# A and B on the sync queue behind the first group of x, B on 32 partitions, and one copy moved: what a shorter setup chain is worth in a LoRA kernel

## Chip, cores and metric

The kernel runs on one core of a Trainium2 chip. The metric is the device time of one execution in microseconds (us). An execution more than 1.5% above the fastest of the same kernel is labelled slow and left out.

## The reference

```python
# x [16, 512, 768], A [768, 16], B [16, 768], all float32; scale = 0.5
lora = np.matmul(np.matmul(x, A), B)
return (x + scale * lora).astype(np.float32)
```

25.2 MB of x come in and 25.2 MB of output go out. A and B have 48 KB each.

## The kernel before

The 8192 rows of x go through in eight groups of 1024. Each partition holds 8 consecutive rows of a group, so a group is 128 pieces of 24,576 bytes. The first six groups are loaded at once into six buffers. The last two wait until stores have freed a buffer. All loads and stores of x are issued on the sync queue (SP), one after another. In the trace of before they land in that order: the loads of the third to the sixth group, issued between 1.39 and 3.17 us, landed 24.2, 30.8, 37.5 and 44.4 us after their issue.

```python
def sync_program():
    ...
    load(0)            # moved into the first block, ahead of the barrier that all engines share
    ...
    for g in range(1, X_BUFS):          # X_BUFS = 6
        load(g)
    for g in range(NG - 1):             # NG = 8
        nc.sync.wait_ge(added, 4 * (g + 1) + 2)
        nc.sync.dma_start(out=view(out2, g), in_=xs[g % X_BUFS]).then_inc(...)
        if g == len(freed) - 1:         # after the second store
            for n in range(X_BUFS, NG):
                nc.sync.wait_ge(freed[n - X_BUFS], 16)
                load(n)
    ...
# last of all:
nc.sync.dma_start(out=view(out2, NG - 1), in_=xs[(NG - 1) % X_BUFS])
```

Per group, ACT casts x to float16, DVE transposes it, PE multiplies by a block form of A (24 matmuls into `y_ps`, "a y pass"), ACT spreads y into diagonal blocks, PE multiplies these by B, and DVE adds the result to x in place.

Before the first group a setup brings A and B into their block forms. A and B are loaded by ACT, behind the barrier:

```python
def scalar_program():
    nc.scalar.dma_start(out=a32, in_=A.rearrange("(p m q) r -> p m (q r)", m=NM, q=2)
                        ).then_inc(a_in, 16)
    nc.scalar.dma_start(out=b32, in_=B).then_inc(b_in, 16)
    ...

def vector_program():
    nc.vector.wait_ge(pool_done, 4)
    nc.vector.tensor_tensor(out=a16, in0=..., in1=..., op=mult     # A, masked
                            )._wait_ge(a_in, 16).then_inc(setup_dve, 1)
    nc.vector.tensor_copy(out=b16[0:R, :], in_=b32)._wait_ge(b_in, 16).then_inc(setup_dve, 1)
    for a in range(NQ): ...            # four copies from PSUM to a_diag
    nc.vector.tensor_copy(out=b_rep, in_=b_ps)._wait_ge(setup_pe, 3).then_inc(added, 2)
    turn(0, 0, G // 2)._wait_ge(ready, 1)          # the first two transposes
    turn(0, G // 2, G // 2)._wait_ge(ready, 2)
    for g in range(NG):
        if g + 1 < NG:
            turn(g + 1, 0, G)._wait_ge(ready, 2 * g + 4)
        for s in range(0, G, 2): ...   # four adds, then the group can be stored
```

Of the kernel before, what the change touches and what calls it, by code (L numbers as in the profile page):

```python
# [1 line left out]

# [7 lines left out]
MM_DT = mybir.dt.float16  # L10
# [4 lines left out]
Q = 32  # L15
# [3 lines left out]
def kernel(  # L19
# [14 lines left out]
    nc = tc.nc  # L34
    fp32 = mybir.dt.float32
    u32 = mybir.dt.uint32
    P = 128
    NQ = P // Q
# [3 lines left out]
    T, D = x2.shape  # L42
    R = A.shape[1]
# [3 lines left out]
    NB = W // Q  # L47
    NM = 4
    PB, PA = Q // NM, W // NM
    assert PA <= P and NM * P <= 512  # L50
    sc = float(scale)

    const = ctx.enter_context(tc.tile_pool(name="const", bufs=1))
    psum = ctx.enter_context(tc.tile_pool(name="psum", bufs=1, space=bass.MemoryType.PSUM))


    x_0 = nc.alloc_sbuf_tensor("x_0", [P, G, D], fp32).ap()
    xs = [x_0] + [const.tile([P, G, D], fp32, name=f"x_{i}") for i in range(1, X_BUFS)]
    xh = [const.tile([P, G, D], MM_DT, name=f"xh_{i}") for i in range(2)]
    xt = const.tile([P, G, W], u32, name="xt")  # L60
    y_diag = const.tile([P, G, P], MM_DT, name="y_diag")


    a32 = const.tile([PA, NM, 2 * R], fp32, name="a32")
    mine = const.tile([PA, NB], MM_DT, name="mine")
    wrap = const.tile([PB, PA], MM_DT, name="wrap")
    step = const.tile([PB, NM, NQ, Q], MM_DT, name="step")
    sel = const.tile([PA, NM, P], MM_DT, name="sel")
    b32 = const.tile([R, D], fp32, name="b32")
    rep = const.tile([Q, NQ * Q], MM_DT, name="rep")  # L70
    a16 = const.tile([PA, NM, NB, 2 * R], MM_DT, name="a16")
    b16 = const.tile([Q, D], MM_DT, name="b16")
    a_diag = const.tile([P, 2 * NB, P], MM_DT, name="a_diag")
    b_rep = const.tile([P, D], MM_DT, name="b_rep")
    y_ps = psum.tile([P, G, Q], fp32, name="y_ps")
    lora_ps = [psum.tile([P, 2, D], fp32, name=f"lora_ps_{i}") for i in range(2)]
# [8 lines left out]
    a_in, b_in = semaphore("a_in"), semaphore("b_in")  # L85
# [17 lines left out]
    def load(g):  # L103
        nc.sync.dma_start(out=xs[g % X_BUFS], in_=view(x2, g)).then_inc(loaded[g], 16)

    def sync_program():
        symbolic, nc._always_lower_symbolic_ap = nc._always_lower_symbolic_ap, False
        load(0)
        nc._always_lower_symbolic_ap = symbolic

        now, first = nc.cur_bb.bb.instructions, nc.main_func.blocks[0].instructions
        at = next(
            k for k, i in enumerate(first)
            if i.engine == mybir.EngineType.SP and isinstance(i, mybir.InstDrain)
        )
        first.insert(at, now.pop())
        for g in range(1, X_BUFS):
            load(g)
        for g in range(NG - 1):
            nc.sync.wait_ge(added, 4 * (g + 1) + 2)  # L120
            nc.sync.dma_start(out=view(out2, g), in_=xs[g % X_BUFS]).then_inc(
                freed[g] if g < len(freed) else stored, 16
            )
            if g == len(freed) - 1:
# [4 lines that stand above are left out]
        nc.sync.wait_ge(added, 4 * NG + 2)  # L129
        nc.sync.sem_clear(range(nums[0], nums[-1] + 1))  # L130

    def pool_program():
        nc.gpsimd.sem_clear(stored)

        nc.gpsimd.memset(rep, 0.0)
        nc.gpsimd.memset(wrap, 0.0)
        nc.gpsimd.memset(step, 0.0)
        nc.gpsimd.memset(mine, 1.0).then_inc(pool_done, 1)
        nc.gpsimd.affine_select(
            out=rep.rearrange("i (a k) -> i a k", a=NQ),  # L140
            in_=rep.rearrange("i (a k) -> i a k", a=NQ),
            compare_op=mybir.AluOpType.not_equal, fill=1.0, base=0,
            pattern=[[0, NQ], [-1, Q]], channel_multiplier=1,
        )._wait_ge(pool_done, 1)

        nc.gpsimd.affine_select(
            out=wrap.rearrange("j (b k) -> j b k", k=PB),
            in_=wrap.rearrange("j (b k) -> j b k", k=PB),
            compare_op=mybir.AluOpType.not_equal, fill=1.0, base=0,
            pattern=[[0, NB], [-1, PB]], channel_multiplier=1,  # L150
        )

        nc.gpsimd.affine_select(
            out=step, in_=step,
            compare_op=mybir.AluOpType.not_equal, fill=1.0, base=0,
            pattern=[[1, NM], [0, NQ], [-1, Q]], channel_multiplier=NM,
        )

        nc.gpsimd.affine_select(
            out=mine, in_=mine, compare_op=mybir.AluOpType.is_ge, fill=0.0, base=0,  # L160
            pattern=[[-PB, NB]], channel_multiplier=1,
        ).then_inc(pool_done, 1)
        nc.gpsimd.affine_select(
            out=mine, in_=mine, compare_op=mybir.AluOpType.is_ge, fill=0.0, base=PB - 1,
            pattern=[[PB, NB]], channel_multiplier=-1,
        )._wait_ge(pool_done, 2).then_inc(pool_done, 1)
        nc.gpsimd.memset(b16, 0.0)
        nc.gpsimd.memset(a_diag, 0.0)
        nc.gpsimd.memset(y_diag, 0.0).then_inc(pool_done, 1)

# [4 lines left out]
        return i  # L175

    def scalar_program():
        nc.scalar.dma_start(
            out=a32, in_=A.rearrange("(p m q) r -> p m (q r)", m=NM, q=2)
        ).then_inc(a_in, 16)  # L180
        nc.scalar.dma_start(out=b32, in_=B).then_inc(b_in, 16)

        nc.scalar.copy(out=sel.rearrange("p m k -> p (m k)"), in_=sel_ps)._wait_ge(
            setup_pe, 1
        ).then_inc(setup_act, 1)
        cast(0, 0, G // 2)._wait_ge(loaded[0], 16)
        cast(0, G // 2, G // 2)
        cast(1, 0, G)._wait_ge(loaded[1], 16)
        for g in range(NG):
            for a in range(NQ):  # L190
                q = ds(a * Q, Q)
                i = nc.scalar.mul(out=y_diag[q, :, q], in_=y_ps[q, :, :], mul=sc)  # L192
                if a == 0:
                    i._wait_ge(ready, min(g + 3, NG + 1) + g + 1)
            i.then_inc(spread, 1)
            if g + 2 < NG:
                cast(g + 2, 0, G)._wait_ge(loaded[g + 2], 16)

    a_ps = lora_ps[0][:, 0, 0 : 2 * NB * R]
    b_ps = lora_ps[1][:, 0, :]  # L200
    sel_ps = lora_ps[0].rearrange("p s d -> p (s d)")[0:PA, 512 : 512 + NM * P]

    def turn(g, s0, n):
        rows = ds(s0, n)
        i = nc.vector.transpose(  # L205
            out=xt[:, rows, :].rearrange("p s w -> p (s w)"),
            in_=xh[g % 2][:, rows, :].rearrange("p s d -> p (s d)").bitcast(u32),
        )
        i.then_inc(turned, 1)
        return i  # L210

    def vector_program():
        nc.vector.wait_ge(pool_done, 4)
        nc.vector.tensor_tensor(  # L214
            out=a16,
            in0=a32[:, :, None, :].to_broadcast([PA, NM, NB, 2 * R]),
            in1=mine[:, None, :, None].to_broadcast([PA, NM, NB, 2 * R]),
            op=mybir.AluOpType.mult,
        )._wait_ge(a_in, 16).then_inc(setup_dve, 1)
        nc.vector.tensor_copy(  # L220
            out=b16[0:R, :], in_=b32
        )._wait_ge(b_in, 16).then_inc(setup_dve, 1)
        for a in range(NQ):
            q = ds(a * Q, Q)
            i = nc.vector.tensor_copy(  # L225
                out=a_diag[q, :, ds(a * Q, R)], in_=a_ps[q, :].rearrange("p (b r) -> p b r", r=R)
            )
            if a == 0:
                i._wait_ge(setup_pe, 2)
        nc.vector.tensor_copy(out=b_rep, in_=b_ps)._wait_ge(setup_pe, 3).then_inc(added, 2)  # L230
        turn(0, 0, G // 2)._wait_ge(ready, 1)
        turn(0, G // 2, G // 2)._wait_ge(ready, 2)
        for g in range(NG):
            if g + 1 < NG:
                turn(g + 1, 0, G)._wait_ge(ready, 2 * g + 4)
            for s in range(0, G, 2):
                n = (g * G + s) // 2
                rows = xs[g % X_BUFS][:, ds(s, 2), :]
                nc.vector.tensor_tensor(  # L239
                    out=rows, in0=rows, in1=lora_ps[n % 2], op=mybir.AluOpType.add  # L240
                )._wait_ge(ups, n + 1).then_inc(added, 1)

    def chunks(c0, n):

        while n:
            k = min(n, 512 - c0 % 512)
            yield c0, k
            c0, n = c0 + k, n - k

    def tensor_program():  # L250
# [9 lines left out]
            if m == 0:  # L260
                i._wait_ge(setup_dve, 1)
        i.then_inc(setup_pe, 1)
        for c0, n in chunks(0, D):
            i = nc.tensor.matmul(
                b_ps[:, ds(c0, n)], rep, b16[:, ds(c0, n)], start=True, stop=True
            )
            if c0 == 0:
                i._wait_ge(setup_dve, 2)
        i.then_inc(setup_pe, 1)
        xt_mm = xt.rearrange("p s w -> p (s w)").bitcast(MM_DT)  # L270
# [69 lines left out]
```

## Time and profile before

| | before |
|---|---|
| time, median of 3 runs | 123.38 us (123.22 to 123.45) |
| span of the profiled run | 121.6 us |
| busy: DVE / ACT / PE | 70% / 46% / 44% |
| sync queue, share of the 16 DMA engines' span | 97.3% |
| last store issued | 109.83 us |

First the page of the kernel before: the DMA rows over the span in 40 slices (tenths busy, then GB/s), the queues (packets, MB, share of the 16 engines), the chain of waits by engine, and one of the issue lines (count, KB each, median us from issue to landing).

```profile
span 121.6 us, 908 instructions
...
DMA  7999999999999999999999999999999999999990
GB/s 234 407 405 409 437 445 404 445 445 404 445 445 404 445 429 421 396 485 412 396 493 404 404 485 404 412 461 421 429 445 412 437 445 412 437 445 412 445 437 40
...
q1 hardware_dynamic: 2304, 50.33, 97.3%
q10 hardware_dynamic: 144, 0.10, 0.3%
...
DVE 51%; PE 28%; DMA 9%; ACT 1%; issue 1%; ACTq 0%; SPq 0%
...
out_dram<-x_61 SPq DMA_DIRECT2D x2, 3072.0 KB, 12.3
```

Queue q1 is the sync queue, q10 is ACT's. The DMA engines are at 9 tenths or more in every slice but the first and the last. The chain of waits nevertheless names DVE and PE and gives the DMA engines 9%. How can both be true? The chain is followed back from the last piece of computing work, and that is the last add. These are its final pieces (start, us, what):

```profile
101.72 0.83 PE lora_ps_82 L289 x4
102.58 6.75 DVE x_61 L239 x4
```

It ends at 109.3 us, and the page follows nothing beyond. The last store and its landing, the remaining 12 us, are not part of it. So this chain says what the last store waits for before it is issued. Here is the issue of the last store (start, us taken, engine, line), then the sync queue's wait for its landing (us in total, times, longest):

```profile
109.83 0.33 SPq L304 DMA_DIRECT2D out_dram<-x_61  x1
...
SPq L335 <- DMA out_dram<-x_61: 10.6, 1, 10.6
```

Last, the setup on DVE from the timeline (start, us, what, and in brackets the idle time before it and what ended it), and below the dots the first y pass on PE:

```profile
11.44 1.75 DVE L214 TENSOR_TENSOR a_77<-a_70,mine 96x1536 f16<-96x1536 f32 x1 [11.44 <-DMA a_70<-in_A_dram]
13.73 0.55 DVE L220 CAST b_78<-b_75 16x768 f16<-16x768 f32 x1 [0.55 <-DMA b_75<-in_B_dram]
14.74 2.26 DVE L225 CAST a_diag<-lora_ps_82 32x384 f16<-32x384 f32 x4 [0.46 <-PE lora_ps_82 L256]
17.01 0.96 DVE L230 CAST b_rep<-lora_ps_83 128x768 f16<-128x768 f32 x1
17.89 3.43 DVE L205 STREAM_TRANSPOSE xt<-xh_66 128x1536 uint32<-128x1536 uint32 x2
...
21.37 5.20 PE L275 MATMUL y_ps<-xt,a_diag 128*128 128x256 f16 x24 [5.92 <-DVE xt L205]
```

So the first y matmul starts at 21.37 us.

### The profile page before, as it was taken

To read this page: it belongs to the slowest core of one execution; us is meant where nothing else is said; L and a number is where in the kernel's file an instruction comes from. 1 tells how busy PE (TensorE), PEld (TensorE's weight loads), DVE (VectorE), ACT (ScalarE), POOL (GpSimd) and SP (SyncE) were. 2 spreads that over 40 slices of the span, in tenths; PEclk is the share of its full clock that TensorE was granted. 3 is DMA by queue.
4 is the path that set the end of the run, shared out by engine and by line. 5 is a ranking of instruction groups with operands and counts; after the bars stand their busy time and mean duration, and the time that the engine had idled before them with its cause. 6 is when DMAs were issued, how large, how long until landed. Compare 5 with 4: busy or idle time off the path is not lost.

```text
span 121.6 us, 908 instructions
## 1 busy us (share of the span) xinstructions
PE 53.3 (44%) x327; PEld 31.3 (26%) x327; DVE 85.6 (70%) x48; ACT 56.5 (46%) x43; POOL 6.8 (6%) x16
## 2 busy tenths in 40 slices
PE   0200600974296449437446742943754594310000
PEld 0000100642154227216213521821432262100000
DVE  0002699029994999999999999999999982990000
ACT  2305929729903990992596299089440004000000
POOL 6950000000000000000000000000000000000000
PEclk9999999999959999999999999999999999985555
DMA  7999999999999999999999999999999999999990
GB/s 234 407 405 409 437 445 404 445 445 404 445 445 404 445 429 421 396 485 412 396 493 404 404 485 404 412 461 421 429 445 412 437 445 412 437 445 412 445 437 40
DMA packets 2448, 50.43 MB, mean 415 GB/s; under 512 B 288, under 2 KB 384, under 8 KB 400
## 3 DMA queue, kind: packets, MB, share of 16 engines
q1 hardware_dynamic: 2304, 50.33, 97.3%
q10 hardware_dynamic: 144, 0.10, 0.3%
HBM read 25.26 MB, written 25.17 MB: 415 GB/s over the span
## 4 chain that ended last, share of the span: by engine, by line
DVE 51%; PE 28%; DMA 9%; ACT 1%; issue 1%; ACTq 0%; SPq 0%
DVE xt L205 22%; PE y_ps L275 20%; DMA a_70<-in_A_dram 9%; DVE x_61 L239 8%; DVE x L239 5%; PE lora_ps_83 L289 5%; DVE x_63 L239 3%; DVE x_62 L239 3%; DVE x_65 L239 3%; DVE x_64 L239 3%; DVE a_diag L225 2%; DVE a_77 L214 1%; ACT y_diag L192 1%; PE lora_ps_82 L256 1%; DVE b_rep L230 1%
## 5 line engine op out<-in xcount | busy, mean ns | idle before, releaser
L275 PE MATMUL y_ps<-xt,a_diag 128*128 128x256 f16 x192 | 26.0, 296 | 5.9 <-DVE xt L205 5.9
L192 ACT ACTIVATE y_diag<-y_ps 32x256 f16<-32x256 f32 x32 | 12.0, 375 | 34.0 <-PE y_ps L275 33.7
L289 PE MATMUL lora_ps_82<-b_rep,y_diag 128*128 128x512 f16 (+1 forms) x64 | 13.2, 328 | 28.4 <-ACT y_diag L192 13.6
L275 PEld LDWEIGHTS y_ps<-xt,a_diag 128*128 128x128 f16 x192 | 19.9, 104 | 12.2 <-DVE xt L205 6.6
L205 DVE STREAM_TRANSPOSE xt<-xh_67 128x3072 uint32<-128x3072 uint32 x4 | 13.5, 3379 | 6.1 <-PE y_ps L275 6.1
L289 PE MATMUL lora_ps_83<-b_rep,y_diag 128*128 128x512 f16 (+1 forms) x64 | 13.7, 339 | 6.7 <-DVE x_61 L239 1.7
L205 DVE STREAM_TRANSPOSE xt<-xh_66 128x3072 uint32<-128x3072 uint32 (+1 forms) x5 | 13.6, 2728 | 2.3 <-PE y_ps L275 2.3
L289 PEld LDWEIGHTS lora_ps_82<-b_rep,y_diag 128*128 128x128 f16 x64 | 4.9, 97 | 35.8 <-issue 15.9
L173 ACT CAST xh_66<-x 128x3072 f16<-128x3072 f32 (+1 forms) x3 | 10.7, 3604 | 5.5 <-DMA x<-in_x_dram 5.5
L173 ACT CAST xh_67<-x_61 128x6144 f16<-128x6144 f32 x2 | 10.6, 5312 | 2.4 <-DMA x_61<-in_x_dram 2.4
L214 DVE TENSOR_TENSOR a_77<-a_70,mine 96x1536 f16<-96x1536 f32 x1 | 1.8, 1753 | 11.4 <-DMA a_70<-in_A_dram 11.4
L289 PEld LDWEIGHTS lora_ps_83<-b_rep,y_diag 128*128 128x128 f16 x64 | 5.7, 100 | 13.1 <-DVE x_61 L239 2.5
L239 DVE TENSOR_TENSOR x_61<-x_61,lora_ps_82 128x1536 f32<-128x1536 f32 x4 | 7.0, 1740 | 2.8 <-PE lora_ps_82 L289 2.8
L239 DVE TENSOR_TENSOR x_61<-x_61,lora_ps_83 128x1536 f32<-128x1536 f32 x4 | 7.0, 1744 | 0.0
L239 DVE TENSOR_TENSOR x<-x,lora_ps_83 128x1536 f32<-128x1536 f32 x4 | 7.0, 1741 | 0.0
L239 DVE TENSOR_TENSOR x<-x,lora_ps_82 128x1536 f32<-128x1536 f32 x4 | 6.9, 1729 | 0.0
L256 PE MATMUL lora_ps_82<-a_77,sel 96*128 96x384 f16 x4 | 1.5, 521 | 8.9 <-DVE a_77 L214 8.9
L173 ACT CAST xh_66<-x_62 128x6144 f16<-128x6144 f32 x1 | 5.3, 5312 | 0.0
L173 ACT CAST xh_67<-x_63 128x6144 f16<-128x6144 f32 x1 | 5.3, 5312 | 0.0
L173 ACT CAST xh_66<-x_64 128x6144 f16<-128x6144 f32 x1 | 5.3, 5312 | 0.0
L173 ACT CAST xh_67<-x_65 128x6144 f16<-128x6144 f32 x1 | 5.3, 5312 | 0.0
L239 DVE TENSOR_TENSOR x_64<-x_64,lora_ps_83 128x1536 f32<-128x1536 f32 x2 | 3.5, 1742 | 0.0
(33 smaller groups left out, 39.5 us busy)
## 6 DMA issues: line engine op xcount, KB each, us to landing
x<-in_x_dram SPq DMA_DIRECT2D x2, 3072.0 KB, 12.5
x_61<-in_x_dram SPq DMA_DIRECT2D x2, 3072.0 KB, 16.1
out_dram<-x SPq DMA_DIRECT2D x2, 3072.0 KB, 16.0
out_dram<-x_61 SPq DMA_DIRECT2D x2, 3072.0 KB, 12.3
x_62<-in_x_dram SPq DMA_DIRECT2D x1, 3072.0 KB, 24.2
x_63<-in_x_dram SPq DMA_DIRECT2D x1, 3072.0 KB, 30.8
x_64<-in_x_dram SPq DMA_DIRECT2D x1, 3072.0 KB, 37.5
x_65<-in_x_dram SPq DMA_DIRECT2D x1, 3072.0 KB, 44.4
```

The lines of the kernel that those rows point to most:

```text
L173: i = nc.scalar.copy(out=xh[g % 2][:, rows, :], in_=xs[g % X_BUFS][:, rows, :])
L192: i = nc.scalar.mul(out=y_diag[q, :, q], in_=y_ps[q, :, :], mul=sc)
L205: i = nc.vector.transpose(out=xt[:, rows, :].rearrange("p s w -> p (s w)"), in_=xh[g % 2][:, rows, :].rearrange("p s d -> p (s d)").bitcas ...
L214: nc.vector.tensor_tensor(out=a16, in0=a32[:, :, None, :].to_broadcast([PA, NM, NB, 2 * R]), in1=mine[:, None, :, None].to_broadcast([PA, ...
L225: i = nc.vector.tensor_copy(out=a_diag[q, :, ds(a * Q, R)], in_=a_ps[q, :].rearrange("p (b r) -> p b r", r=R))
L230: nc.vector.tensor_copy(out=b_rep, in_=b_ps)._wait_ge(setup_pe, 3).then_inc(added, 2)
L239: nc.vector.tensor_tensor(out=rows, in0=rows, in1=lora_ps[n % 2], op=mybir.AluOpType.add)._wait_ge(ups, n + 1).then_inc(added, 1)
L256: i = nc.tensor.matmul(a_ps, sel[:, m, :], a16[:, m].rearrange("p b r -> p (b r)"), start=(m == 0), stop=(m == NM - 1),)
L275: i = nc.tensor.matmul(y_ps, a_diag[:, k, :], xt_mm[:, :, k // 2, :, k % 2], start=(k == 0), stop=(k == 2 * NB - 1),)
L289: i = nc.tensor.matmul(flat[:, ds(c0, w)], y_diag[:, s + k, :], b_rep[:, ds(c0 - k * D, w)], start=True, stop=True,)
```

## The change

The intent is to shorten this setup. A and B come in behind the first group of x on the same queue, ahead of the barrier. B lies on 32 partitions above A's 96, half a row in each, so its cast is shorter and its two matmuls are equal. The copy to `b_rep` goes behind the first two transposes. The core of the diff:

```diff
+    H = 2
+    HB = P - H * R
+    ab = nc.alloc_sbuf_tensor("ab", [P, D // H], fp32).ap()
-    a32 = const.tile([PA, NM, 2 * R], fp32, name="a32")
+    a32 = ab[0:PA, 0 : NM * 2 * R].rearrange("p (m r) -> p m r", m=NM)
-    b32 = const.tile([R, D], fp32, name="b32")
-    rep = const.tile([Q, NQ * Q], MM_DT, name="rep")
+    b32 = ab[HB:, 0 : D // H]
+    take = const.tile([P, H, NQ, Q], MM_DT, name="take")
 ...
     def sync_program():
-        ... load(0) moved into the first block ...
+        with ahead(mybir.EngineType.SP):       # moves what is issued here into the first block
+            load(0)
+            nc.sync.dma_start(
+                out=a32, in_=A.rearrange("(p m q) r -> p m (q r)", m=NM, q=2)
+            ).then_inc(a_in, 16)
+            nc.sync.dma_start(
+                out=b32, in_=B.rearrange("r (h c) -> (r h) c", h=H)
+            ).then_inc(b_in, 16)
 ...
-        nc.gpsimd.memset(b16, 0.0)
 ...
     def scalar_program():
-        nc.scalar.dma_start(out=a32, ...).then_inc(a_in, 16)
-        nc.scalar.dma_start(out=b32, in_=B).then_inc(b_in, 16)
 ...
     def vector_program():
-        nc.vector.tensor_copy(out=b16[0:R, :], in_=b32)...
+        nc.vector.tensor_copy(out=b16[HB:], in_=b32)...
 ...
-        nc.vector.tensor_copy(out=b_rep, in_=b_ps)._wait_ge(setup_pe, 3).then_inc(added, 2)
         turn(0, 0, G // 2)._wait_ge(ready, 1)
         turn(0, G // 2, G // 2)._wait_ge(ready, 2)
+        nc.vector.tensor_copy(
+            out=b_rep.rearrange("p (h c) -> p h c", h=H), in_=b_ps
+        )._wait_ge(setup_pe, 3).then_inc(added, 2)
 ...
-        for c0, n in chunks(0, D):             # 512 and 256 columns
-            i = nc.tensor.matmul(b_ps[:, ds(c0, n)], rep, b16[:, ds(c0, n)], ...)
+        for h in range(H):                     # 384 columns each
+            i = nc.tensor.matmul(b_ps[:, h, :], take[HB:, h]..., b16[HB:], ...)
```

More of the change, by code (lines that the diff above doesn't have):

```diff
@@ L1 @@
-from contextlib import ExitStack
+from contextlib import ExitStack, contextmanager
 import concourse.bass as bass
@@ L49 @@
     PB, PA = Q // NM, W // NM
-    assert PA <= P and NM * P <= 512
+    H = 2
+    HB = P - H * R
+    assert PA <= HB == 3 * Q and NM * P <= 512 and NM * 2 * R <= D // H <= 512
     sc = float(scale)
@@ L68 @@
     sel = const.tile([PA, NM, P], MM_DT, name="sel")
-    b32 = const.tile([R, D], fp32, name="b32")
-    rep = const.tile([Q, NQ * Q], MM_DT, name="rep")
+    b32 = ab[HB:, 0 : D // H]
+    take = const.tile([P, H, NQ, Q], MM_DT, name="take")
     a16 = const.tile([PA, NM, NB, 2 * R], MM_DT, name="a16")
-    b16 = const.tile([Q, D], MM_DT, name="b16")
+    b16 = const.tile([P, D // H], MM_DT, name="b16")
     a_diag = const.tile([P, 2 * NB, P], MM_DT, name="a_diag")
@@ L104, in load, with ahead, sync_program @@
         nc.sync.dma_start(out=xs[g % X_BUFS], in_=view(x2, g)).then_inc(loaded[g], 16)
-    def sync_program():
+    @contextmanager
+    def ahead(engine):
         symbolic, nc._always_lower_symbolic_ap = nc._always_lower_symbolic_ap, False
-        load(0)
+        now, first = nc.cur_bb.bb.instructions, nc.main_func.blocks[0].instructions
+        old = len(now)
+        yield
         nc._always_lower_symbolic_ap = symbolic
-        now, first = nc.cur_bb.bb.instructions, nc.main_func.blocks[0].instructions
         at = next(
             k for k, i in enumerate(first)
-            if i.engine == mybir.EngineType.SP and isinstance(i, mybir.InstDrain)
+            if i.engine == engine and isinstance(i, mybir.InstDrain)
         )
-        first.insert(at, now.pop())
+        while len(now) > old:
+            first.insert(at, now.pop())
+    def sync_program():
+        with ahead(mybir.EngineType.SP):
[6 more added lines that the diff above has]
+            ).then_inc(b_in, 16)
         for g in range(1, X_BUFS):
@@ L133, in pool_program @@
         nc.gpsimd.sem_clear(stored)
-        nc.gpsimd.memset(rep, 0.0)
+        nc.gpsimd.memset(take[HB:], 0.0)
         nc.gpsimd.memset(wrap, 0.0)
@@ L139, in pool_program @@
         nc.gpsimd.affine_select(
-            out=rep.rearrange("i (a k) -> i a k", a=NQ),
-            in_=rep.rearrange("i (a k) -> i a k", a=NQ),
+            out=take[HB:], in_=take[HB:],
             compare_op=mybir.AluOpType.not_equal, fill=1.0, base=0,
-            pattern=[[0, NQ], [-1, Q]], channel_multiplier=1,
+            pattern=[[-1, H], [0, NQ], [-H, Q]], channel_multiplier=1,
         )._wait_ge(pool_done, 1)
@@ L177, in scalar_program @@
     def scalar_program():
-        nc.scalar.dma_start(
-            out=a32, in_=A.rearrange("(p m q) r -> p m (q r)", m=NM, q=2)
-        ).then_inc(a_in, 16)
-        nc.scalar.dma_start(out=b32, in_=B).then_inc(b_in, 16)
         nc.scalar.copy(out=sel.rearrange("p m k -> p (m k)"), in_=sel_ps)._wait_ge(
@@ L199 @@
     a_ps = lora_ps[0][:, 0, 0 : 2 * NB * R]
-    b_ps = lora_ps[1][:, 0, :]
+    b_ps = lora_ps[1].rearrange("p s d -> p (s d)")[:, 0 : H * 512]
+    b_ps = b_ps.rearrange("p (h c) -> p h c", h=H)[:, :, 0 : D // H]
     sel_ps = lora_ps[0].rearrange("p s d -> p (s d)")[0:PA, 512 : 512 + NM * P]
@@ L220, in vector_program @@
         nc.vector.tensor_copy(
-            out=b16[0:R, :], in_=b32
+            out=b16[HB:], in_=b32
         )._wait_ge(b_in, 16).then_inc(setup_dve, 1)
@@ L262, in tensor_program @@
         i.then_inc(setup_pe, 1)
-        for c0, n in chunks(0, D):
+        for h in range(H):
             i = nc.tensor.matmul(
-                b_ps[:, ds(c0, n)], rep, b16[:, ds(c0, n)], start=True, stop=True
+                b_ps[:, h, :], take[HB:, h].rearrange("p a k -> p (a k)"), b16[HB:],
+                start=True, stop=True,
             )
-            if c0 == 0:
+            if h == 0:
                 i._wait_ge(setup_dve, 2)
```

## The prediction

> **What bounds the kernel now.** The DMA engines. The queue table gives the sync queue, which carries all of x in and out, 97.3% of the 16 engines' span; the slice rows show DMA at 9 in all slices but the first and last. The packet records of the trace agree: 16 packets of 24,576 bytes are in flight nearly throughout, each takes 912 ns, and a 3.15 MB group needs 7.26 us, about 433 GB/s. [...] An engine moves 128 such packets: 128 x 0.912 = 116.7 of the 121.6 us (estimate). DVE is busy 70%, PE 44%.
>
> The chain of waits looks different: it starts with A's load (10.45 us, 9%), then DVE and PE. But it ends with the last add at 109.3 us; the last store is issued at 109.83 (timeline), while by the packet records the store before it occupies the engines until about 113 us. So the last store comes about 3 us before the engines could begin it. The first store, issued at about 35 us, likewise stands behind loads that end at about 47.5.
>
> **What the change does.**
> - A and B leave the ACT queue, where their packets took turns with those of x (one 512-byte packet of A per 0.93 us x packet), and follow x_0 in the sync queue. Before: x_0 seen at 10.47 us, A at 11.44, B about 13.7. After (estimate): about 10.3, 10.7, 10.9.
> - Three sync issues instead of one ahead of the barrier, about 0.4 us each: the other engines start about 0.8 us later. Pool's setup, which ended at 7.84, loses a 0.73 us memset, so still ends before A. The issue of x_1 moves from 1.0 to about 1.8, long before x_0 is through.
> - B's cast is 32x384 instead of 16x768: about 0.28 us, not 0.55. Two 384-column matmuls for 512 + 256: equal work.
> - The 0.96 us copy to b_rep goes behind the first two transposes and runs while PE computes y.
>
> So the compute chain gains about 0.7 us from A and 0.96 us from b_rep: the first y matmul at about 19.7 instead of 21.37, every add about 1.7 us earlier, the last ending at about 107.6.
>
> **How much is on the critical path.** Almost none. The bytes are the same and the engines stay full. The last store is issued at about 108.1 and lands when it did: its time to landing grows from 12.3 to about 14 us. What can change is what A and B cost the DMA engines: before, the stage of x_1 took 7.73 us instead of 7.26. Without the taking of turns that could be 0.1 to 0.3 us less; small packets in line could equally leave a bubble.
>
> **Prediction:** 123.2 us, range 122.6 to 123.8. Faster by over 2%: 2%. Within 2%: 96%. Slower by over 2%: 2%.
>
> **What would show it right or wrong.** Waits: DVE waits for A until about 10.7 us. Timeline: first y matmul near 19.7, last store issued near 108. Issues table: last store's landing near 14 us. Queue table: sync queue still at 97%. If the y matmul is earlier but the span unchanged, "bound by DMA" holds; if the span falls by over 1 us, it fails.
>
> **What would make it wrong.** Stores at the end not queued as I read them; small packets behind x_0 stalling the engines by over 0.5 us; the later barrier delaying x_1 enough for a gap; the slow first packets (1.2 to 2.3 us instead of 0.91) changing with the issue order.

## The result, and the profile after

| | before | after |
|---|---|---|
| time, median of 4 runs each | 123.37 us (123.22 to 123.45) | 123.19 us (123.04 to 123.28) |
| span of the profiled run | 121.6 us | 121.2 us |
| DVE starts on A | 11.44 us | 10.63 us |
| first y matmul | 21.37 us | 19.70 us |
| last store issued | 109.83 us | 107.49 us |
| sync queue waits for its landing | 10.6 us | 12.6 us |

The ratio is 0.9986, with a 95% interval of 0.9968 to 1.0003. Ratios here are the mean time of one kernel's fast runs over that of the other's of the same rounds, so they are not quite the ratio of the medians. The output is correct. The interval includes 1.

The page of the changed kernel:

```profile
span 121.2 us, 907 instructions
...
DMA  7999999999999999999999999999999999999992
GB/s 227 414 398 421 438 438 422 430 438 422 414 454 422 406 470 422 406 446 446 406 430 462 406 430 446 422 430 438 430 430 438 422 438 438 422 438 438 422 438 89
...
q1 hardware_dynamic: 2464, 50.43, 97.9%
...
DVE 50%; PE 27%; DMA 8%; ACT 1%; issue 1%; SPq 0%
```

ACT's queue is gone and the sync queue carries its 0.10 MB. The busy rows are the same picture. Now the setup on DVE and the first y pass, from the timeline of the changed kernel:

```profile
10.63 1.75 DVE L228 TENSOR_TENSOR a<-ab,mine 96x1536 f16<-96x1536 f32 x1 [10.63 <-DMA ab<-in_A_dram]
12.41 0.35 DVE L234 CAST b<-ab 32x384 f16<-32x384 f32 x1
13.94 2.25 DVE L239 CAST a_diag<-lora_ps 32x384 f16<-32x384 f32 x4 [1.17 <-PE lora_ps L272]
16.21 3.44 DVE L219 STREAM_TRANSPOSE xt<-xh 128x1536 uint32<-128x1536 uint32 x2
19.68 0.96 DVE L246 CAST b_rep<-lora_ps 128x768 f16<-128x768 f32 x1
...
19.70 4.74 PE L292 MATMUL y_ps<-xt,a_diag 128*128 128x256 f16 x24 [5.05 <-DVE xt L219]
```

A is there 0.81 us earlier. B's cast takes 0.35 instead of 0.55 us and waits for no load. The copy to `b_rep` follows the transposes, beside the first y pass. And the sync queue at the end, its issue of the last store from the timeline and then its wait for the landing:

```profile
107.49 0.33 SPq L321 DMA_DIRECT2D out_dram<-x  x1
...
SPq L352 <- DMA out_dram<-x: 12.6, 1, 12.6
```

The store is issued 2.34 us earlier and then waited for 2.0 us longer. So the gain of the chain has become time in the queue.

The packet records of both traces say the same. They are not printed here. Counted from the first packet of x (1.0 us after the start of the span), the packets of the last store but one end at 111.61 us before and 111.49 after. The DMA engines were not free for the last store any earlier than that, whenever it was issued.

### The profile page after: what moved, and what is told of

It reads as the page before. It is cut to its first block, busy times and chain, and to the rows that moved or that the text cites. A ratio compares the mean times of both kernels' runs of the same rounds, so it can differ in the third digit from the quotient of the medians.

```text
span 121.2 us, 907 instructions
## 1 busy us (share of the span) xinstructions
PE 52.6 (43%) x327; PEld 31.0 (26%) x327; DVE 85.5 (71%) x48; ACT 56.5 (47%) x43; POOL 6.5 (5%) x15
## 4 chain that ended last, share of the span: by engine, by line
DVE 50%; PE 27%; DMA 8%; ACT 1%; issue 1%; SPq 0%
DVE x L255 25%; DVE xt L219 22%; PE y_ps L292 20%; DMA ab<-in_A_dram 8%; PE lora_ps L306 6%; DVE a_diag L239 2%; DVE a L228 1%; ACT y_diag L205 1%; PE lora_ps L272 1%; SPq L109 0%
## 5 line engine op out<-in xcount | busy, mean ns | idle before, releaser
L255 DVE TENSOR_TENSOR x<-x,lora_ps 128x1536 f32<-128x1536 f32 x32 | 53.7, 1737 | 2.8 <-PE lora_ps L306 2.8
L190 ACT CAST xh<-x 128x6144 f16<-128x6144 f32 (+1 forms) x9 | 42.6, 4744 | 7.1 <-DMA x<-in_x_dram 7.0
L306 PE MATMUL lora_ps<-b_rep,y_diag 128*128 128x512 f16 (+1 forms) x128 | 25.6, 334 | 35.1 <-DVE x L255 21.5
L219 DVE STREAM_TRANSPOSE xt<-xh 128x3072 uint32<-128x3072 uint32 (+1 forms) x9 | 27.1, 3018 | 6.7 <-PE y_ps L292 6.7
L306 PEld LDWEIGHTS lora_ps<-b_rep,y_diag 128*128 128x128 f16 x128 | 10.7, 99 | 48.9 <-DVE x L255 27.6
L228 DVE TENSOR_TENSOR a<-ab,mine 96x1536 f16<-96x1536 f32 x1 | 1.8, 1753 | 10.6 <-DMA ab<-in_A_dram 10.6
L272 PE MATMUL lora_ps<-a,sel 96*128 96x384 f16 x4 | 1.5, 521 | 6.7 <-DVE a L228 6.7
L239 DVE CAST a_diag<-lora_ps 32x384 f16<-32x384 f32 x4 | 2.2, 553 | 1.2 <-PE lora_ps L272 1.2
L185 POOL MEMSET a_diag<- 128x3072 f16 x1 | 2.7, 2655 | 0.0
L246 DVE CAST b_rep<-lora_ps 128x768 f16<-128x768 f32 x1 | 1.0, 958 | 0.0
```

The lines of the kernel that those rows point to most:

```text
L185: nc.gpsimd.memset(a_diag, 0.0)
L190: i = nc.scalar.copy(out=xh[g % 2][:, rows, :], in_=xs[g % X_BUFS][:, rows, :])
L219: i = nc.vector.transpose(out=xt[:, rows, :].rearrange("p s w -> p (s w)"), in_=xh[g % 2][:, rows, :].rearrange("p s d -> p (s d)").bitcas ...
L228: nc.vector.tensor_tensor(out=a16, in0=a32[:, :, None, :].to_broadcast([PA, NM, NB, 2 * R]), in1=mine[:, None, :, None].to_broadcast([PA, ...
L239: i = nc.vector.tensor_copy(out=a_diag[q, :, ds(a * Q, R)], in_=a_ps[q, :].rearrange("p (b r) -> p b r", r=R))
L246: nc.vector.tensor_copy(out=b_rep.rearrange("p (h c) -> p h c", h=H), in_=b_ps)._wait_ge(setup_pe, 3).then_inc(added, 2)
```

## The experiments

Theory: the DMA engines bound the kernel. They are fed far enough ahead that a setup chain 2 us shorter only makes the stores wait longer in the queue. Rival 1: the chain bounds, and the change gave its gain back through new costs (the later barrier, small packets in line with large ones). Rival 2: the chain bounds and there is no new cost, so the gain should be seen.

Twelve runs were made, in three sets. Each set ran on one chip, together with the kernel before.

### The change again, and each part alone

The change was repeated in five rounds.

> The changed kernel as it is, in five rounds. Theory (bound by the DMA engines, the gain of the compute chain lies in slack): ratio to before 0.997 to 1.001. Rival (the chain of waits is what bounds, and new costs ate its gain of about 2 us): the same time, but then the DMA engines should show idle stretches that before did not have, of some 2 us. A chain that bounds with no new cost: ratio 0.98.

It measured 123.45 us (123.02 to 123.87) against 123.41 us of before, ratio 1.001 (0.9992 to 1.0029). The first comparison's 0.14% did not come again. With both, no difference is shown. The DMA row of its page is at 9 in all slices but the first and the last, and the queue's share is 97.8%: the idle stretches that rival 1 asks for are not there.

**The copy alone.** The kernel before, with one line moved:

```diff
-        nc.vector.tensor_copy(out=b_rep, in_=b_ps)._wait_ge(setup_pe, 3).then_inc(added, 2)
         turn(0, 0, G // 2)._wait_ge(ready, 1)
         turn(0, G // 2, G // 2)._wait_ge(ready, 2)
+        nc.vector.tensor_copy(out=b_rep, in_=b_ps)._wait_ge(setup_pe, 3).then_inc(added, 2)
```

> The kernel before with nothing changed but the order on DVE: the copy to b_rep behind the first two transposes. Theory: the first y matmul starts about 0.96 us earlier than before's 21.37, near 20.4, the last store is issued about 1 us earlier, near 108.9, and the time stays at 1.000 (0.998 to 1.002). If the chain bound: ratio 0.992.

Measured: 123.29 us, ratio 0.9993 (0.9979 to 1.0007). The first y matmul came at 20.70, not 20.4, since A was seen 0.19 us later in this run than in before's (11.63). From A's start to the first y matmul it took 9.07 us instead of 9.93, so the copy is worth 0.86 us there. The last store was issued at 110.36 us, later than in before, against the expectation. The reason follows below the table.

**The queue alone.** The kernel before, with A and B moved to the sync queue and B as it was:

```diff
+        with ahead(mybir.EngineType.SP):
             load(0)
+            nc.sync.dma_start(out=a32, in_=A.rearrange(...)).then_inc(a_in, 16)
+            nc.sync.dma_start(out=b32, in_=B).then_inc(b_in, 16)
 ...
-        nc.scalar.dma_start(out=a32, ...).then_inc(a_in, 16)
-        nc.scalar.dma_start(out=b32, in_=B).then_inc(b_in, 16)
```

> The kernel before with A and B loaded by the sync queue behind the first group of x, ahead of the barrier, B on 16 partitions as before. Theory: DVE starts on A near 10.65 us instead of 11.44, the first y matmul near 20.6 instead of 21.37, the last store is issued near 109.0; the time within 0.3% of before, and if the whole change is really 0.1% faster, this part has that (0.998 to 1.000). If small packets in line stalled the engines: the group of x after them would take over 8.2 us instead of 7.7 and the time 0.5 us more.

Measured: 123.27 us, ratio 0.9993 (0.9977 to 1.001). A was seen at 10.64 us and the first y matmul came at 20.58, as expected. The last store was issued at 106.79 us, 2.2 us earlier than expected; the reason is the same as for the copy. The group of x behind the small packets took 7.83 us by the packet records, not over 8.2: no stall. Without ACT's queue the bytes took as long as with it (123.27 against 123.41 us).

**The layout alone.** The changed kernel, with the loads back on ACT and the copy back in its place:

```diff
-            nc.sync.dma_start(out=a32, ...) ; nc.sync.dma_start(out=b32, ...)
+        nc.scalar.dma_start(out=a32, ...) ; nc.scalar.dma_start(out=b32, ...)   # behind the barrier
 ...
+        nc.vector.tensor_copy(out=b_rep..., in_=b_ps)...
         turn(0, 0, G // 2)._wait_ge(ready, 1)
         turn(0, G // 2, G // 2)._wait_ge(ready, 2)
-        nc.vector.tensor_copy(out=b_rep..., in_=b_ps)...
```

> The changed kernel with A and B back on the ACT queue behind the barrier and the copy to b_rep back ahead of the transposes, so only B's place on 32 partitions and its two equal matmuls are new. Theory: B's cast falls from 0.55 to 0.35 us, but it runs beside the four matmuls of A, so the first y matmul stays within 0.2 us of before's 21.37 and the time at 0.999 to 1.001.

Measured: 123.31 us, ratio 1.0 (0.9981 to 1.0018). The first y matmul came at 21.48. B's cast took 0.36 us, but DVE waited 1.28 us for B before it (0.55 in before), since B was seen later (14.34 instead of 13.73 us). The layout by itself gains nothing.

Here are the profiled, fast runs side by side. "Landed" is the issue plus its 0.33 us plus the wait that follows, all three read from the sync queue's timeline and waits:

| kernel | first y matmul | last store issued | waited for | landed | time of that run |
|---|---|---|---|---|---|
| before | 21.37 | 109.83 | 10.6 | 120.8 | 123.44 |
| copy alone | 20.70 | 110.36 | 9.9 | 120.6 | 123.24 |
| layout alone | 21.48 | 107.65 | 12.4 | 120.4 | 123.03 |
| queue alone | 20.58 | 106.79 | 13.5 | 120.6 | 123.26 |
| changed kernel | 19.70 | 107.49 | 12.6 | 120.4 | 123.04 |
| changed kernel again | 19.57 | 106.56 | 13.5 | 120.4 | 123.02 |

The issue varies by 3.8 us, while the landing varies by 0.4 us and does not follow the issue. That is what a full queue looks like.

Why does the issue not follow the first y matmul? The y passes of the first groups take different times from run to run. The first pass (24 matmuls) took 4.24 us in one of these runs and 5.30 us in another, the second 2.84 to 4.20, while in all these runs the fourth and later ones took 2.84 (2.83 in some). Here are the PEclk row (granted clock in tenths, over 40 slices; it shows 9 also before the first record) and the first y passes of the copy-alone run, then the same of the queue-alone run:

```profile
PEclk9999999999959967999999999999999999998555
...
20.70 5.30 PE L275 MATMUL y_ps<-xt,a_diag 128*128 128x256 f16 x24 [5.05 <-DVE xt L205]
33.71 4.20 PE L275 MATMUL y_ps<-xt,a_diag 128*128 128x256 f16 x24
45.94 3.25 PE L275 MATMUL y_ps<-xt,a_diag 128*128 128x256 f16 x24
...
PEclk9999999999999999999999999999999999955555
...
20.58 4.49 PE L284 MATMUL y_ps<-xt,a_diag 128*128 128x256 f16 x24 [5.92 <-DVE xt L214]
32.51 2.84 PE L284 MATMUL y_ps<-xt,a_diag 128*128 128x256 f16 x24
```

The clock records of the traces of before and of the changed kernel are not printed here. The first of them, at full clock, starts 4.95 us after the first y matmul in before and 4.01 us after it in the changed kernel. Their first passes took 5.20 and 4.74 us, so full clock is recorded near the end of each, at moments 0.9 us apart counted from the pass. What sets the moment is not shown.

The records show one thing more. In both traces the clock later fell back to 0.5 once before the last y pass, for 3.41 us. By the PEclk rows of the pages it fell back once in the repeat of the changed kernel (a 5), twice in the copy-alone run (a 5, then a 6 and a 7), and not at all in the queue-alone and layout-alone runs. Every second or third pass that was slow overlaps such a stretch (in before 33.15 to 36.56 us, with the second pass from 34.60; in the changed kernel 30.54 to 33.95 us, with the second pass from 32.47), and no other was slow. So the copy-alone run had the slow passes (5.30, 4.20, 3.25 us), the queue-alone run the fast ones (4.49, 2.84, 2.84 us). The passes account for 2.6 of the 3.6 us between the two issues.

The same kernel twice shows as much: the two profiles of the changed kernel with half stores, which come below, issued their last store at 108.59 (a run labelled slow) and 105.64 us, with the first y matmul at 19.96 and 19.82. The chain's end thus moves by some 3 us from run to run, more than the change moves it.

### What moving the bytes costs by itself

The changed kernel without any computing: a store waits only for its own load. Its output is wrong, which doesn't matter for the time.

```diff
-            nc.sync.wait_ge(added, 4 * (g + 1) + 2)
+            if g == 0:
+                nc.sync.wait_ge(pool_done, 1)
+            nc.sync.wait_ge(loaded[g], 16)
 ...
-        pool_program()
-        scalar_program()
-        vector_program()
-        tensor_program()
+        nc.gpsimd.sem_clear(stored)
+        nc.gpsimd.memset(mine, 1.0).then_inc(pool_done, 1)
```

> The changed kernel without any compute, wrong on purpose: the same loads and stores of x, and of A and B, in the same order on the sync queue; a store waits for its load alone. It measures what moving the bytes costs by itself. Theory: 122.9 to 123.2 us, within 0.3 us of the changed kernel, so that all the compute together adds next to nothing. Rival (the chain bounds): clearly less, below 121 us.

It measured 123.22 us (122.83 to 124.54), ratio 0.9994 (0.9947 to 1.0041), a hair above the range that was expected. Its page:

```profile
span 122.0 us, 73 instructions
...
DMA  6999999999999999999998999999999999999990
```

The same loads and stores without one matmul or add take the same time. So all the computing of the changed kernel costs nothing that shows within that interval (half a per cent either way), and shortening it cannot gain more than that while the bytes go this way.

### Fewer bytes

If the DMA engines hide the gain, it must come out when they have less to do. Both kernels were run with stores of only the first four of the eight rows that a partition holds. Their outputs are wrong, which doesn't matter for the times. The same edit was made to the final store:

```diff
-            nc.sync.dma_start(out=view(out2, g), in_=xs[g % X_BUFS]).then_inc(
+            nc.sync.dma_start(
+                out=view(out2, g)[:, 0 : G // 2, :], in_=xs[g % X_BUFS][:, 0 : G // 2, :]
+            ).then_inc(
```

> The kernel before, wrong on purpose: each store writes only the first four of the eight rows that a partition holds, so the DMA engines move 37.8 MB instead of 50.4 and have time to spare, while all the compute stays. Estimate: the bytes need about 91 us with the start; the last add still ends near 109, then half a store of about 5 us: span about 115.8, time about 117.7 us (0.954 of before). If the DMA engines did not bound the whole kernel, the time would fall by much less than 4 us.

> The changed kernel with the same half stores, wrong on purpose. Theory: with the DMA engines out of the way, the chain bounds, and the change shows its gain: 1.7 to 2.4 us under the half-store version of before (about 115.5 us, ratio of the two 0.980 to 0.986). Rival (the gain of the chain is eaten by new costs of the change): the two half-store kernels within 0.5 us of each other.

The first pair, on a chip with much spread, gave medians of 118.01 and 115.66 us over all runs. The ratios of the fast runs to the kernel before were 0.9423 and 0.9288, so the pair's own ratio is 0.9857. Its fast means are 116.31 and 114.65 us, 1.7 us apart, within what was expected of the pair. The medians lie near the 117.7 and 115.5 us that were expected, the fast means below them. The pair was repeated with five more rounds. It had been meant for another chip but came to the same one.

> The half-store version of before once more on another chip, since the first pair ran on one whose times spread by several us. The last store should be issued at 109 to 111.5 us; the time 115.5 to 117 us.

> The half-store version of the changed kernel once more. Theory: 1.3 to 2.2 us under the half-store version of before, as the first pair gave 1.7; the first y matmul about 1.7 us earlier in the two profiles. Rival (the gain of the chain is eaten by new costs): within 0.5 us.

The repeat gave 117.30 and 114.62 us over all runs. The ratios were 0.9427 and 0.9195, the fast means 116.40 and 113.46 us, 2.9 us apart. That is more than the 2.2 expected at most. The half-store version of before had its median just above the expected 117 us, and its profiled run, a slow one, issued the last store at 111.91, above the expected 111.5. The first y matmul came 1.7 us earlier in the first pair's profiles (21.68 and 19.96) and 1.8 in the second's (21.62 and 19.82), as expected. In the fast runs of both pairs together (six of each) the changed kernel is 2.3 us faster. The label does not make this difference: over all twelve runs of each, slow ones included, the means are 117.83 and 115.19 us, 2.6 us apart. Part of it goes with the clock: among fast runs with a granted clock of 0.964 to 0.970 it is 1.9 us (three runs at 115.78 on average against five at 113.83). An effect of about 2 us, where the theory expected 1.7 to 2.4, and nothing like the 0.5 at most of rival 1. The page of the changed kernel with half stores (the repeat, a fast run), with the sync queue's wait for the last landing:

```profile
span 111.5 us, 907 instructions
...
DMA  7999999999999999899999999999501910580085
...
q1 hardware_dynamic: 2464, 37.85, 81.0%
...
SPq L356 <- DMA out_dram<-x: 4.7, 1, 4.7
```

From about seven tenths of the span on, the DMA engines stand idle between stores. Now the chain bounds, and now the change is worth its 2 us. Both profiled runs of the half-store version of before were slow ones, so their last stores are not compared. Rival 1 falls here: new costs of the change would have eaten its gain in this pair too.

### More chain

The opposite test lengthens the chain of the changed kernel until the queue runs dry. The masked multiplication of A was repeated 2 or 6 times ahead of the true one, and the result stays right:

```diff
+        for again in range(2):          # 6 in the other kernel
+            i = nc.vector.tensor_tensor(out=a16, in0=..., in1=..., op=mybir.AluOpType.mult)
+            i._wait_ge(lag if again else a_in, again or 16).then_inc(lag, 1)
         nc.vector.tensor_tensor(
             out=a16, ...
-        )._wait_ge(a_in, 16).then_inc(setup_dve, 1)
+        )._wait_ge(lag, 2).then_inc(setup_dve, 1)
```

> The changed kernel with the multiplication that makes the masked A repeated twice more ahead of the true one, some 3.6 us of added work at the head of the chain; the result stays right. Theory: the last store is issued near 111.1 us instead of 107.49, still before the engines are through with the store ahead of it (about 113), so the time grows by less than 0.4 us. Rival (the chain bounds): 3.6 us more, ratio to before about 1.03.

This expectation was half missed. The runs spread from 123.37 to 125.85 us, median 124.52. The four fast ones gave a ratio of 1.0042 (0.9995 to 1.0089). Two executions cost nothing (123.37 and 123.39 us), others up to 2.5 us. The profiled run was the slowest. Its y passes of the second and third groups took 5.12 and 3.73 us, against 3.55 and 2.83 in the changed kernel's profile, so its last store was issued at 114.24 instead of 111.1 us. There the delay and the slow passes together were more than the slack. That run is labelled slow, so it explains one execution. What I had not counted is the chance part of the chain.

> Six added multiplications, some 10.7 us at the head of the chain. Theory: the slack of 3 to 6 us is used up and the rest shows: last store issued near 118 us, time 128.5 to 131 us, 5 to 8 us above before, that is well under the 10.7 added. Rival (the chain bounds): 133 us or more.

Measured: 130.17 us (127.88 to 132.31), correct; the median is within what was expected. Only two of the six runs are labelled fast. The profiled run (129.47 us, fast) had the same y passes as the changed kernel's profile (4.74, 3.55, 2.84 us), so the two compare directly. The last store was issued at 118.25, which is 10.76 us later. The span is only 6.7 us longer. The page, and the sync queue's wait for the last landing:

```profile
span 127.9 us, 913 instructions
...
DMA  7999999999999989509898989999999999997893
GB/s 238 430 433 389 438 423 438 423 438 430 438 423 438 423 377 484 254 0 492 369 369 369 492 377 384 392 430 446 415 438 423 438 438 423 438 423 315 369 476 138
...
q1 hardware_dynamic: 2464, 50.43, 94.1%
...
SPq L361 <- DMA out_dram<-x: 8.4, 1, 8.4
```

My expectation thought of the last store alone. The row shows more: a slice with 0 GB/s near 55 us. There the six loads and the first store were done and the second store, issued at 56.9 us, was not there yet. By the packet records that group took 12.1 us instead of 7.3. Of the 6.6 us lost, 4.8 arose there. Another 1.1 arose in the last load, some of whose packets took up to 1.95 us (why is not shown), and 0.8 at the end, where the engines again stood idle before the last store. The wait of 8.4 us is therefore what an unqueued store of a whole group takes to land after its issue. It is the same 8.4 us in the run with two delays. This gives a measure of the slack: the wait in any run, less 8.4. In the profiles of before and after it is 10.6 - 8.4 = 2.2 and 12.6 - 8.4 = 4.2 us. The change added 2.0 us of slack and no speed.

### The start of the transfers

What the bytes leave is the start: the first 16 packets took 1.68 us on average in the changed kernel, later ones 0.91. The last experiment loads the first group in two halves:

```diff
-            load(0)
+            for s in (0, G // 2):
+                nc.sync.dma_start(
+                    out=x_0[:, ds(s, G // 2), :], in_=view(x2, 0)[:, ds(s, G // 2), :]
+                ).then_inc(loaded[0], 16)
 ...
-        cast(0, 0, G // 2)._wait_ge(loaded[0], 16)
+        cast(0, 0, G // 2)._wait_ge(loaded[0], 32)
```

> The changed kernel with the first group of x loaded as two transfers of four rows, so that the first packets have 12,288 bytes. The bytes alone take what the changed kernel takes, so the start is where something may be left: the first packets took 1.4 to 2.2 us where later ones take 0.91. If that excess grows with the packet, 0.2 to 0.5 us are won (ratio to before 0.995 to 0.998); if it is a fixed delay, nothing (0.998 to 1.001).

It measured 123.19 us against 123.48 of before, ratio 0.9976 (0.9956 to 0.9996). By the number alone that falls into the first branch of the expectation, but the trace does not bear it out. The first packets, half as large, took 0.99 us, but the first group was complete 8.68 us after the first packet, against 8.74 and 8.66 in the two profiles of the changed kernel. Where 0.24% would come from is not shown in the trace, and the kernel did not run beside the changed one, whose medians were 123.19 and 123.45 us. It is not shown to beat it.

## Why the prediction was right

- **What bounds the kernel: right.** The bytes alone took 123.22 us. With fewer of them the change was worth about 2 us, with all of them nothing that is shown.
- **The chain's gain: right in its parts.** Expected were A at about 10.7 us and the first y matmul at about 19.7; measured were 10.63 and 19.70. Alone, the queue brought A forward by 0.80 us and the copy saved 0.86 us. The layout, which the prediction valued at nothing on the chain, brought nothing.
- **The end of the chain: somewhat under-sized.** 1.7 us earlier was predicted and 2.3 measured. The rest came from y passes of 4.74 and 3.55 us instead of 5.20 and 3.78, which vary by chance. The prediction had no term for that, and it is larger than the gain itself.
- **The slack at the end: right in kind, smaller.** The prediction put it at about 3 us, from the issue at 109.83 to about 113. In the trace the packets before it end at 112.62, and the prediction left out that the first packet follows 0.83 to 0.84 us after the start of an issue (measured on the last stores of the two delayed kernels, which did not queue). That leaves 2.0 us; measured by the waits it was 2.2. The first store was issued at 36.65 us, not about 35, still well before the loads end at 47.1.
- **The last store's landing: right in its change, wrong in its level.** The prediction read 12.3 us as the landing of the last store. That line has x2: its figure is the median of two stores from that buffer. The last one alone took 0.33 + 10.6 = 10.9 us before, and 12.9 after instead of about 14. The growth of 2.0 us is what counts.
- **Cheaper transfers of A and B, 0.1 to 0.3 us: not shown.** The stage of the second group of x took 7.73 us before and 7.82 after, the first group 8.97 and 8.74. Together that is 0.14 us less, which is within what repeats of the same kernel differ by (16.56 and 16.40 us for both groups).
- **The later barrier: as expected.** The three issues ahead of it took 0.38, 0.42 and 0.43 us, and the second group of x was issued at 1.93 instead of 1.01 us. That did no harm, since the first group held the engines until about 10 us.
- **The size of B's cast** was 0.35, not 0.28 us (an estimate, half of the 0.55 before), off the chain. The two matmuls behind it took 0.51 us each on average in both traces, as "equal work" has it.

Still open: on one chip two executions of the kernel before were slow (125.31 and 125.58 us, granted clock 0.900). Whether the larger slack of the changed kernel makes such executions rarer was not tested.

## What to carry to other kernels

A chain of waits that ends with the last computation says what the last store waits for. It does not say whether the transfer engines would have been free for it; look also at the busy row of the DMA and at how long a store is waited for after its issue, and subtract what an unqueued one takes. Here, while that difference was above zero, earlier work only added slack. A run of the transfers alone and a run with fewer bytes settle it within one set of experiments. A part of the chain that varies by chance has to be counted against the slack as well.

## What else the traces show

- With one core at work, 3.15 MB stores followed each other every 7.27 us and loads every 7.31 us by the packet records of before, which is 433 and 430 GB/s.
- In the trace of before the 96 packets of A, each 512 bytes, were spread over 4.8 us (5.28 to 10.09 us) beside the packets of x, each 24,576 bytes: up to 9.0 us, 16 of them moved every 0.93 us. In the changed kernel they passed within 0.9 us (9.04 to 9.93 us), in line behind the first group. So the small load arrived earlier in line than beside the large one: DVE started on A at 10.63 instead of 11.44 us. The first packet of A beside x moved only at 5.28 us, 4.3 us after its issue; why is not shown.
- The first 16 packets of the changed kernel took 1.4 to 2.2 us each where later ones of the same size take 0.91, and the first group of x took about 1.4 us more than a later one (8.7 instead of 7.3 us).
- In the six runs of the table the first y pass took 1.4 to 2.5 us longer than the later ones (4.24 to 5.30 against 2.84), which is 1.2 to 2.0% of the 121 us of the span. Together with the slow second and third passes it moved the end of the compute chain by about 3 us of 107 between runs, though not the time: the last store's issue came at 110.36 with the slow passes and at 106.79 with the fast ones, although the first y matmul differed by only 0.1 us.
